# Down in 25 blocks whose lengths begin at five, its first operands asked for two groups ahead, no sum loaded at first visits, x2 added at last visits

## The chip, the cores and the metric

The kernel runs on one core of a Trainium2 chip. The metric is the device time of one execution in microseconds; lower is better. Before the change the median of three runs is 1912.93 us (1912.73 to 1913.06).

## What is computed

A decoder layer on 512 positions of width 2048, all in float32. The change is in the last line, in the product with `w_down`:

```python
D_MODEL = 2048; SEQ = 512; DEPTH = 1
D_FF = -(-(8 * D_MODEL) // (3 * 256)) * 256          # 5632
...
h = _rms_norm(x, norm1_g[l])
proj = h @ w_in[l]                                   # three head groups of token mixing
...
x = x + mix @ w_out[l]                               # x2 in the kernel
h2 = _rms_norm(x, norm2_g[l])
x = x + (jax.nn.silu(h2 @ w_gate[l]) * (h2 @ w_up[l])) @ w_down[l]
```

## The kernel before

Everything is held transposed: tiles of 128 channels x 512 positions. Four stages follow each other: the input projection, the mixers with the output projection (they leave x2 in DRAM, `x2d`, 16 tiles), gate/up, and down. Matmuls run in float32r, and each weight tile is split into a rounded part `wh` and a rest `wl`; an operand tile holds the rounded half and the rest side by side.

Gate/up and down multiply 2x2 blocks with **seven products instead of eight** (`ORDER = (5, 1, 7, 6, 2, 4, 3)`). A group is one output pair: seven products, each over a number of operand pairs `j`, each pair one `wh` matmul over 512 columns and one `wl` matmul over 256. A weight group has four raw blocks `'21'`, `'22'`, `'11'`, `'12'`; POOL adds them (L178), ACT copies the sum to PSUM (`wn`, L230) and to `wh` (L231), DVE subtracts for `wl` (L232), two products ahead of PE, with three `wh`/`wl` buffers. Four PSUM banks take the products; DVE evicts each product after it (L949, L954, L955), in `done`.

Gate/up has 44 groups (g0, u0, g1, u1, ...; pairs in the order `GU_ORDER`), eight operand pairs each; the 56 operand tiles `h` stay in SBUF. After a `u` group POOL forms sums and ACT and DVE make seven operand tiles of this pair (`piece1` to `piece4`, called in the next groups by `later`), which SP stores to DRAM (`od`). The pairs in `STAY` also stay in SBUF, and the second of them is not stored.

Down contracts over 44 row tiles, 22 pairs, for 16 output tiles (8 pairs `n` and `n + 8`). The operand tiles of all 22 pairs don't fit into the 75 slots of 128x512, so down runs as a list of **blocks** `DOWN`, each `(n, first, end)`: output pair n over operand pairs first to end - 1 (modulo 22). Before, there are 24: each n is visited three times, the window of operand pairs slides up by about one pair a block, and the list starts with lengths 6, 7, 7 and ends with seven of 7. A block's products are seven as in gate/up. At each visit SP loads the running sums of n and n + 8 (`y`, from `x2d`, so that x2 is in them from the start), DVE and POOL add the products, and SP stores the sums back to `x2d`, at the last visit to the output.

The order is written out by hand. Each engine's queue runs in the order of the program; there is no scheduler. `later(k, f, queue=extras)` puts a call at the end of the product k further on. SP issues nearly every DMA, in order: weights (`pump`, up to seven raw buffers), operands (`load_act`), sums (`load_y`), stores. A DMA into a slot waits until the slot's last reader is done, and what stands behind it on SP waits too.

Of the kernel before, what the change touches and what calls it, by code (L numbers as in the profile page):

```python
# [9 lines left out]
F32 = mybir.dt.float32  # L10
# [5 lines left out]
P = 128  # L16
T = 512
NT = T // P
D = 2048
KT = D // P  # L20
# [41 lines left out]
ORDER = (5, 1, 7, 6, 2, 4, 3)  # L62
TH = T // 2
NJ = KT // 2
NP = NF // 2


GU_ORDER = [*range(1, 6), *range(7, NP), 0, 6]
STAY = (0, 6)


_A = [0, 0, 1, 2, 3, 4, 5, 6]
_B = [_A[n] + (6 if n == 0 else 7) for n in range(8)]
_C = [b + 8 for b in _B]
DOWN = [(n, *w) for ab in (zip(_A, _B), zip(_B, _C), zip(_C, [a + NP for a in _A])) for n, w in enumerate(ab)]

LAID = (5, 7, 6, 4, 3, 1, 2)

# [35 lines left out]
def kernel(ctx: ExitStack, tc: tile.TileContext, xT, wi, wo, wgu, wd, cst_in, outT):  # L114
    nc = tc.nc
# [18 lines left out]
    def slot(name, dt=F32, cols=T):  # L134
        return sp.tile([P, cols], dt, name=name, tag="s")
# [625 lines left out]
    for name in PROJ[HEAD4:]:  # L761
        kind, what, j = name[0], name[1], name[2:]
# [3 lines left out]
        b = project(name)  # L766
# [19 lines left out]
    b = box = boxes = shared = None  # L786

    x2 = {}
# [168 lines left out]
    class Wide(Block):  # L957
# [6 lines left out]
        def done(self, q):  # L964
            if q == 1:
                self.u = slot(f"{self.name}u")
                self.u1, self.u2 = halves(self.u)
                self.both(1, self.u1)
            elif q == 7:
                self.l, self.r = slot(f"{self.name}l"), slot(f"{self.name}r")  # L970
                self.both(7, self.r[:, :TH])
                self.add(5, self.r[:, :TH], sign=nc.vector.tensor_sub)
            elif q == 6:
                self.add(6, self.u2, self.u1)
                nc.gpsimd.tensor_sub(self.r[:, :TH], self.r[:, :TH], self.u2)
# [65 lines left out]


    y = {}

    def load_y(t):
        if t < len(DOWN):
            for n in (DOWN[t][0], DOWN[t][0] + 8):
                y[t, n] = slot(f"y{t}_{n}")
                nc.sync.dma_start(y[t, n], x2d[n])

    class Down(Block):


        def __init__(self, t):
            super().__init__(f"d{t}", t % 2)
            self.n = DOWN[t][0]
            self.out = outT if t >= 16 else x2d
            self.tail = t == len(DOWN) - 1
            self.y1, self.y2 = y.pop((t, self.n)), y.pop((t, self.n + 8))

        def store(self, n, t, cols):
            def go():
# [6 lines left out]
        def done(self, q):  # L1069
            one, two = slice(0, TH), slice(TH, T)  # L1070
            if q == 1:
                self.u = slot(f"{self.name}u")
                self.u1, self.u2 = halves(self.u)
                self.both(1, self.u1)
            elif q == 7:
                self.add(7, self.y2[:, two])
                self.add(5, self.y2[:, two], sign=nc.vector.tensor_sub)
            elif q == 6:
                self.add(6, self.u2, self.u1)
                nc.gpsimd.tensor_sub(self.y2[:, two], self.y2[:, two], self.u2)  # L1080
                nc.gpsimd.tensor_sub(self.y2[:, one], self.y2[:, one], self.u2)
                nc.gpsimd.tensor_add(self.y1[:, two], self.y1[:, two], self.u2)
                self.u = self.u1 = self.u2 = None
                self.store(self.n + 8, self.y2, two)
            elif q != 5:
                t, n, cols = {2: (self.y1, self.n, one), 4: (self.y2, self.n + 8, one), 3: (self.y1, self.n, two)}[q]
                self.add(q, t[:, cols])
                self.store(n, t, cols)

    def load_act(q, pairs):  # L1090
        for j in pairs:
            if (q, j) in acts or j == STAY[1]:
                continue
            acts[q, j] = slot(f"a{q}_{j}", F32R)
            at = LAID.index(q)
            nc.sync.dma_start(acts[q, j].bitcast(F32), od[j % NP][:, at * T:(at + 1) * T])

    blk = gate = None
    for g in range(2 * NP + len(DOWN)):
        t = g - 2 * NP  # L1100
        if t < 0:
            p, m = GU_ORDER[g // 2], g % 2
            blk = Wide(p, m, gate if m else None)
            gate = blk if m == 0 else None
        else:
            n, first, end = DOWN[t]
            blk = Down(t)
        for i, q in enumerate(ORDER):
# [24 lines left out]
            run(extras)  # L1133
# [85 lines left out]
```

## Time and profile before

| | us |
|---|---|
| median of three runs | 1912.93 |
| the profiled execution, its own time | 1913.02 |
| its span, first to last instruction | 1911.2 |
| PE busy | 1889.6 |
| DVE, ACT, POOL busy | 1441.7, 1323.7, 1165.1 |
| down, from its first matmul to its last | 1469.25 to 1907.5 |

Lines are those of the kernel before. In a row `wl<-w('s', 'd0')_14950,wn`, d0 is the first down block, g6 and u6 the last gate and up group, 's' the buffer of the weight sum; `a` is an operand tile of down, `out` a PSUM bank, `y` a running sum. L941 is the matmul of gate/up and down.

### The profile page before, as it was taken

To read this page: it belongs to the slowest core of one execution; us is meant where nothing else is said; L and a number is where in the kernel's file an instruction comes from. 1 tells how busy PE (TensorE), PEld (TensorE's weight loads), DVE (VectorE), ACT (ScalarE), POOL (GpSimd) and SP (SyncE) were. 2 spreads that over 40 slices of the span, in tenths; PEclk is the share of its full clock that TensorE was granted. 3 is DMA by queue.
4 is the path that set the end of the run, shared out by engine and by line. 5 is a ranking of instruction groups with operands and counts; after the bars stand their busy time and mean duration, and the time that the engine had idled before them with its cause. 6 is when DMAs were issued, how large, how long until landed. Compare 5 with 4: busy or idle time off the path is not lost.

```text
span 1911.2 us, 29738 instructions
## 1 busy us (share of the span) xinstructions
PE 1889.6 (99%) x10332; PEld 1639.4 (86%) x10332; DVE 1441.7 (75%) x2408; ACT 1323.7 (69%) x1836; POOL 1165.1 (61%) x794
## 2 busy tenths in 40 slices
PE   8999999999999999999999999999999999999999
PEld 7888888878887888888888888888888788888888
DVE  6788888896469777777777777777777677767776
ACT  6355654454356888888878888888887677767675
POOL 5134423331056888787878878787876666556564
PEclk9999999999999999999999999999999999999999
DMA  7233333333442344454434444444438788777685
GB/s 266 85 127 93 89 103 96 94 89 118 136 144 83 127 162 148 142 179 139 175 128 165 166 160 144 153 167 146 168 127 299 271 286 281 248 261 262 211 270 195
DMA packets 135974, 320.29 MB, mean 168 GB/s; under 512 B 15504, under 2 KB 30992, under 8 KB 135824
## 3 DMA queue, kind: packets, MB, share of 16 engines
q1 hardware_dynamic: 135680, 318.30, 49.1%
q8 instruction: 81, 1.33, 0.3%
q14 instruction: 69, 0.57, 0.1%
q10 hardware_dynamic: 144, 0.10, 0.0%
HBM read 255.42 MB, written 55.31 MB: 163 GB/s over the span
## 4 chain that ended last, share of the span: by engine, by line
PE 96%; DMA 2%; DVE 1%; POOL 1%; issue 0%; SPq 0%; ACT 0%; POOLq 0%; ACTq 0%; DVEq 0%
PE out L941 66%; PE o L249 3%; PE o L251 3%; PE o L250 3%; PE cq L249 2%; PE cq L251 2%; PE cq L250 2%; PE ak L249 1%; PE ak L251 1%; PE ak L250 1%; PE av L251 1%; PE av L249 1%; PE av L250 1%; PE aq L249 1%; PE aq L250 1%; PE aq L251 1%
## 5 line engine op out<-in xcount | busy, mean ns | idle before, releaser
L941 PE MATMUL out<-h,wh 128*128 128x512 f32 x2464 | 590.2, 391 | 0.9 <-DVE h L809 0.9
L941 PEld LDWEIGHTS out<-h,wh 128*128 128x128 f32 x2464 | 453.7, 189 | 89.1 <-DVE h L809 1.4
L941 PEld LDWEIGHTS out<-h,wl 128*128 128x128 f32 x2464 | 316.1, 191 | 12.1
L941 PE MATMUL out<-h,wl 128*128 128x256 f32 x2464 | 320.0, 283 | 0.0
L941 PE MATMUL out<-a,wh 128*128 128x512 f32 x1232 | 297.8, 392 | 4.0 <-DMA a<-od 2.8
L941 PEld LDWEIGHTS out<-a,wh 128*128 128x128 f32 x1232 | 226.3, 189 | 49.8 <-DMA a<-od 5.0
L226 ACT CAST wh<-w 128x1024 fp32r<-128x1024 f32 (+1 forms) x93 | 96.9, 1042 | 121.3 <-PE o L250 52.6
L941 PEld LDWEIGHTS out<-a,wl 128*128 128x128 f32 x1232 | 160.2, 192 | 8.1 <-DMA a<-od 1.5
L941 PE MATMUL out<-a,wl 128*128 128x256 f32 x1232 | 163.0, 284 | 0.9 <-DMA a<-od 0.9
L227 DVE TENSOR_TENSOR wl<-w,wh 128x1024 fp32r<-128x1024 f32 (+1 forms) x93 | 116.0, 1247 | 54.0 <-ACT wh L226 52.1
L954 DVE TENSOR_TENSOR y<-y,out 128x256 f32<-128x256 f32 x120 | 50.5, 421 | 63.4 <-PE out L941 60.4
L426 DVE SCALAR_TENSOR_TENSOR y<-bu,cst,y 128x511 f32<-128x511 f32 (+14 forms) x120 | 89.8, 749 | 0.6
L955 DVE TENSOR_TENSOR y<-y,out 128x256 f32<-128x256 f32 x120 | 50.5, 421 | 4.1
L250 PE MATMUL o<-ml_c,wh 128*128 128x512 f32 x128 | 50.3, 393 | 2.5 <-DVE ml_c L740 2.5
L249 PE MATMUL o<-mh_c,wh 128*128 128x512 f32 x128 | 51.5, 402 | 0.0
L249 PE MATMUL cq<-hh,wh 128*128 128x512 f32 x128 | 51.2, 400 | 0.0
L251 PE MATMUL o<-mh_c,wl 128*128 128x512 f32 x128 | 50.2, 392 | 0.0
L251 PE MATMUL cq<-hh,wl 128*128 128x512 f32 x128 | 50.0, 391 | 0.0
L250 PE MATMUL cq<-hl,wh 128*128 128x512 f32 x128 | 49.9, 390 | 0.0
L836 POOL TENSOR_TENSOR ta<-h 128x256 f32<-128x256 f32 x8 | 7.3, 908 | 58.5 <-issue 44.9
L348 POOL TENSOR_TENSOR ssum<-ssum,sq 128x512 f32<-128x512 f32 x15 | 25.1, 1675 | 21.9 <-ACT sq L347 21.4
L654 POOL TENSOR_SCALAR a3e<-a3e,a3d 128x128 f32<-128x128 f32 (+3 forms) x8 | 9.1, 1150 | 36.8 <-DVE a3d L652 27.3
(3097 smaller groups left out, 4958.8 us busy)
## 6 DMA issues: line engine op xcount, KB each, us to landing
a<-od SPq DMA_DIRECT2D x182, 256.0 KB, 5.3
od<-a SPq DMA_DIRECT2D x147, 256.0 KB, 3.2
w<-in_wi SPq DMA_DIRECT2D x59, 512.0 KB, 3.7
w<-in_wo SPq DMA_DIRECT2D x32, 512.0 KB, 3.6
y<-x2d SPq DMA_DIRECT2D x48, 256.0 KB, 5.2
x2d<-y SPq DMA_DIRECT2D x64, 128.0 KB, 3.2
x<-in_xT SPq DMA_DIRECT2D x16, 256.0 KB, 7.0
xr<-in_xT SPq DMA_DIRECT2D x16, 256.0 KB, 3.7
```

The lines of the kernel that those rows point to most:

```text
L226: nc.scalar.copy(hi[:, :n], t[:, :n])
L227: eng.tensor_sub(lo[:, :n], t[:, :n], hi[:, :n].bitcast(F32))
L249: nc.tensor.matmul(out, wh, xh, start=start, stop=False)
L250: nc.tensor.matmul(out, wh, xl, start=False, stop=False)
L251: nc.tensor.matmul(out, wl, xh, start=False, stop=stop)
L348: eng.tensor_add(acc, acc, sq)
L426: nc.vector.scalar_tensor_tensor(yconv[j][:, i:], hconv[j][:, :T - i], c, yconv[j][:, i:], op0=ALU.mult, op1=ALU.add)
L654: nc.gpsimd.tensor_scalar(e[:, o:o + n], e[:, o:o + n], rd[:, i:i + 1], None, op0=ALU.mult)
L836: eng.tensor_sub(n1, h11, h12)
L941: nc.tensor.matmul(out, lhs[:, s], rhs, start=begin, stop=last and low == flip[0] and x is xs[-1], skip_group_check=True)
L954: sign(out, out if first is None else first, main)
L955: sign(out, out, rest)
```

## The change

It replaces the list of blocks, and what is loaded, added and stored with them.

- `DOWN` has 25 blocks: (0,0,5), (1,0,6), (2,0,7), (3,0,8), (4,1,9) to (7,4,12), then eight of length 8 from (0,5,13) to (7,12,20), then (0,13,18), (3,16,22), (2,15,22), (1,14,22), (4,17,23) to (7,20,26) of six, and (0,18,22) of four. n = 0 is visited four times. The pairs summed over are the same 176.
- The order is no longer a sliding window, so `FROM` and `UP_TO` say which operand pairs are still or already needed at each block. The operands of 24 pairs are loaded instead of 26.
- The first block has five operand pairs, of which pair 0 stays. Its loads for products 5 and 1 are asked in the gate group before the last (`t == -2`), the others one product after another in the last one; the last of them falls into d0's first product.
- A first visit loads no sum; its evictions write the sum tiles. Sums between visits are in DRAM tiles of their own (`yd`). At a last visit SP loads x2 as well, and POOL adds it to the loaded sum, called at the block's second product.
- `piece2` of each gate/up pair is called one product later. `STAY` is (0, 5), and `GU_ORDER` ends with 0, 5.

The diff, without what only renames:

```diff
+_A = [0, 0, 0, 0, 1, 2, 3, 4]
+_B = [n + 5 for n in range(8)]
+_C = [n + 13 for n in range(8)]
...
+DOWN += [(0, 13, 18), *((n, 13 + n, NP + _A[n]) for n in (3, 2, 1, 4, 5, 6, 7)), (0, 18, NP)]
+FROM = [min(w[1] for w in DOWN[t:]) for t in range(len(DOWN))]
+UP_TO = [max(end, 21 if n == 0 and 13 <= first else 0) for n, first, end in DOWN]
...
-                                     (5, self.piece2), (8, self.piece4)):
+                                     (6, self.piece2), (8, self.piece4)):
...
     def load_y(t):
         if t < len(DOWN):
-            for n in (DOWN[t][0], DOWN[t][0] + 8):
-                y[t, n] = slot(f"y{t}_{n}")
-                nc.sync.dma_start(y[t, n], x2d[n])
+            k = DOWN[t][0]
+            for n in (k, k + 8):
+                if t > FIRST[k]:
+                    y[t, n] = slot(f"y{t}_{n}")
+                    nc.sync.dma_start(y[t, n], yd[n])
+                if t == LAST[k]:
+                    x2[n] = slot(f"x2_{n}")
+                    nc.sync.dma_start(x2[n], x2d[n])
...
-            self.out = outT if t >= 16 else x2d
+            self.out = outT if t == LAST[self.n] else yd
...
+            if t == LAST[self.n]:
+                for n, into in zip(pair, (self.y1, self.y2)):
+                    later(1, nc.gpsimd.tensor_add, into, into, x2.pop(n), queue=extras)
...
             elif q == 7:
-                self.add(7, self.y2[:, two])
+                if self.first:
+                    self.both(7, self.y2[:, two])
+                else:
+                    self.add(7, self.y2[:, two])
...
+                if not self.first:
+                    nc.gpsimd.tensor_sub(self.y2[:, one], self.y2[:, one], self.u2)
+                    nc.gpsimd.tensor_add(self.y1[:, two], self.y1[:, two], self.u2)
...
+            if t == -2 and i in (3, 6):
+                load_act(ORDER[i // 6], range(*DOWN[0][1:]))
             if t == -1:
                 for j in range(NJ):
                     ops.pop((q, j))
-                later(1, load_act, q, range(*DOWN[0][1:]), queue=extras)
+                if i < len(ORDER) - 2:
+                    later(1 if i < len(ORDER) - 3 else 3, load_act, ORDER[i + 2], range(*DOWN[0][1:]), queue=extras)
             elif 0 <= t < len(DOWN) - 1:
-                for j in range(first, DOWN[t + 1][1]):
+                for j in range(FROM[t], FROM[t + 1]):
                     acts.pop((q, j))
-                later(1, load_act, q, range(end, DOWN[t + 1][2]), queue=extras)
+                later(1, load_act, q, range(UP_TO[t], UP_TO[t + 1]), queue=extras)
```

On SP, between the weights of the last up group and those of d0, before (a5_0 is the operand tile of product 5, pair 0; od0 its DRAM tile):

```order
L213 DMA w('12', 'u6')_14694<-in_wgu 128x1024
L915 DMA od0_5893<-a3_0_14679 128x512
L915 DMA od0_5893<-a1_0_14682 128x512
L915 DMA od0_5893<-a5_0_14745 128x512
L915 DMA od0_5893<-a7_0_14748 128x512
L915 DMA od0_5893<-a6_0_14807 128x512
L915 DMA od0_5893<-a4_0_14810 128x512
L213 DMA w('21', 'd0')_14851<-in_wd 128x768
```

and now:

```order
L921 DMA od0_5893<-a1_0_14698 128x512
L1128 DMA a5_1_14759<-od1_5894 128x512
L1128 DMA a5_2_14761<-od2_5895 128x512
L1128 DMA a5_3_14763<-od3_5896 128x512
L1128 DMA a5_4_14765<-od4_5897 128x512
L921 DMA od0_5893<-a5_0_14769 128x512
L921 DMA od0_5893<-a7_0_14772 128x512
L1128 DMA a1_1_14854<-od1_5894 128x512
L1128 DMA a1_2_14856<-od2_5895 128x512
L1128 DMA a1_3_14858<-od3_5896 128x512
L1128 DMA a1_4_14860<-od4_5897 128x512
L219 DMA w('21', 'd0')_14881<-in_wd 128x640
```

Eight operand loads have moved ahead of d0's weights, and the stores of a6_0 and a4_0 behind them. The loads of d0's product 3 (a3_1 and on) stand behind d1's '21', '22' and '11' in both.

On ACT, while d0 and the start of d1 run, before (u6ta and u6tb are sums of the last pair; wn and wh the copies of a weight):

```order
L230 CAST wn407_15232<-w('s', 'd0')_14950 128x768
L231 CAST wh407_15230<-w('s', 'd0')_14950 128x768
L230 CAST wn408_15255<-w('s', 'd1')_15188 128x896
L231 CAST wh408_15253<-w('s', 'd1')_15188 128x896
L1016 CAST u6n2_15271<-u6tb_15136 128x512
L1020 CAST a6_6_15273<-u6tb_15136 128x256
L1020 CAST a4_6_15276<-u6tb_15136 128x256
L230 CAST wn409_15284<-w('11', 'd1')_15111 128x896
L231 CAST wh409_15282<-w('11', 'd1')_15111 128x896
```

and now:

```order
L236 CAST wn407_15217<-w('s', 'd0')_14978 128x640
L237 CAST wh407_15215<-w('s', 'd0')_14978 128x640
L236 CAST wn408_15237<-w('s', 'd1')_15182 128x768
L237 CAST wh408_15235<-w('s', 'd1')_15182 128x768
L236 CAST wn409_15256<-w('11', 'd1')_15113 128x768
L237 CAST wh409_15254<-w('11', 'd1')_15113 128x768
L1022 CAST u5n2_15270<-u5tb_15134 128x512
L1026 CAST a6_5_15272<-u5tb_15134 128x256
L1026 CAST a4_5_15275<-u5tb_15134 128x256
```

The weight copies are shorter by one pair, and `piece2` stands one product later.

On POOL, at the last visit of n = 2 (d18 in both), before:

```order
L1082 TENSOR_TENSOR y17_1_18407<-y17_1_18407,d17u_18546 128x256
L178 TENSOR_TENSOR w('s', 'd18')_18573<-w('s', 'd18')_18573,w('11', 'd18')_18505 128x896
L178 TENSOR_TENSOR w('s', 'd18')_18573<-w('s', 'd18')_18573,w('12', 'd18')_18554 128x896
L178 TENSOR_TENSOR w('s', 'd19')_18769<-w('21', 'd19')_18693,w('22', 'd19')_18696 128x896
L178 TENSOR_TENSOR w('21', 'd19')_18693<-w('21', 'd19')_18693,w('11', 'd19')_18699 128x896
```

and now (L921 is the line that runs a queued call):

```order
L1103 TENSOR_TENSOR y17_3_18383<-y17_3_18383,d17u_18511 128x256
L184 TENSOR_TENSOR w('s', 'd18')_18533<-w('s', 'd18')_18533,w('11', 'd18')_18473 128x896
L921 TENSOR_TENSOR y18_2_18557<-y18_2_18557,x2_2_18559 128x512
L921 TENSOR_TENSOR y18_10_18561<-y18_10_18561,x2_10_18563 128x512
L184 TENSOR_TENSOR w('s', 'd18')_18533<-w('s', 'd18')_18533,w('12', 'd18')_18519 128x896
```

Two additions of x2 have come in between the two later sums of this block's weights.

More of the change, by code (lines that the diff above doesn't have):

```diff
@@ L65 @@
 NP = NF // 2
[L68 to L75, printed above, removed]
+GU_ORDER = [*range(1, 5), *range(6, NP), 0, 5]
+STAY = (0, 5)
+_A = [0, 0, 0, 0, 1, 2, 3, 4]
+_B = [n + 5 for n in range(8)]
+_C = [n + 13 for n in range(8)]
+DOWN = [(n, *w) for ab in (zip(_A, _B), zip(_B, _C)) for n, w in enumerate(ab)]
+DOWN += [(0, 13, 18), *((n, 13 + n, NP + _A[n]) for n in (3, 2, 1, 4, 5, 6, 7)), (0, 18, NP)]
+FROM = [min(w[1] for w in DOWN[t:]) for t in range(len(DOWN))]
+UP_TO = [max(end, 21 if n == 0 and 13 <= first else 0) for n, first, end in DOWN]
+UP_TO = [max(UP_TO[:t + 1]) for t in range(len(DOWN))]
+LAST = {n: t for t, (n, _, _) in enumerate(DOWN)}
+FIRST = {n: t for t, (n, _, _) in reversed([*enumerate(DOWN)])}
 LAID = (5, 7, 6, 4, 3, 1, 2)
@@ L1043 @@
     y = {}
+    yd = {n: tc.dram_tile([P, T], F32, name=f"yd{n}") for n in range(KT)}
     def load_y(t):
         if t < len(DOWN):
-            for n in (DOWN[t][0], DOWN[t][0] + 8):
-                y[t, n] = slot(f"y{t}_{n}")
-                nc.sync.dma_start(y[t, n], x2d[n])
+            k = DOWN[t][0]
[6 more added lines that the diff above has]
+                    nc.sync.dma_start(x2[n], x2d[n])
     class Down(Block):
@@ L1056, in __init__ @@
             self.n = DOWN[t][0]
-            self.out = outT if t >= 16 else x2d
+            self.out = outT if t == LAST[self.n] else yd
             self.tail = t == len(DOWN) - 1
-            self.y1, self.y2 = y.pop((t, self.n)), y.pop((t, self.n + 8))
+            self.first = t == FIRST[self.n]
+            pair = (self.n, self.n + 8)
+            self.y1, self.y2 = [slot(f"y{t}_{n}") if self.first else y.pop((t, n)) for n in pair]
+            if t == LAST[self.n]:
+                for n, into in zip(pair, (self.y1, self.y2)):
+                    later(1, nc.gpsimd.tensor_add, into, into, x2.pop(n), queue=extras)
         def store(self, n, t, cols):
@@ L1080, in done @@
                 nc.gpsimd.tensor_sub(self.y2[:, two], self.y2[:, two], self.u2)
-                nc.gpsimd.tensor_sub(self.y2[:, one], self.y2[:, one], self.u2)
-                nc.gpsimd.tensor_add(self.y1[:, two], self.y1[:, two], self.u2)
-                self.u = self.u1 = self.u2 = None
+                if not self.first:
+                    nc.gpsimd.tensor_sub(self.y2[:, one], self.y2[:, one], self.u2)
+                    nc.gpsimd.tensor_add(self.y1[:, two], self.y1[:, two], self.u2)
+                    self.u = self.u1 = self.u2 = None
                 self.store(self.n + 8, self.y2, two)
@@ L1086, in done @@
                 t, n, cols = {2: (self.y1, self.n, one), 4: (self.y2, self.n + 8, one), 3: (self.y1, self.n, two)}[q]
-                self.add(q, t[:, cols])
+                out = t[:, cols]
+                if not self.first:
+                    self.add(q, out)
+                elif q == 2:
+                    self.both(q, out)
+                elif q == 3:
+                    self.add(q, out, self.u2)
+                    self.u = self.u1 = self.u2 = None
+                else:
+                    main, rest = halves(self.banks[q])
+                    nc.vector.tensor_sub(out, main, self.u2)
+                    nc.vector.tensor_add(out, out, rest)
                 self.store(n, t, cols)
@@ L1091, in load_act @@
         for j in pairs:
-            if (q, j) in acts or j == STAY[1]:
+            if j in STAY or (q, j) in acts:
                 continue
```

## The prediction

> **What bounds the kernel now.** I read the page first, then the waits of PE, the stage by windows, the chain, and SP's timeline. PE is busy almost the whole span, so only its idle time and its slow stretches can be won.
>
> ```profile
> span 1911.2 us, 29738 instructions
> PE 1889.6 (99%) x10332; PEld 1639.4 (86%) x10332; DVE 1441.7 (75%) x2408; ACT 1323.7 (69%) x1836; POOL 1165.1 (61%) x794
> ```
>
> The waits of PE from 1400 us on, which is the end of gate/up and all of down, are two rows:
>
> ```profile
> PE out L941 <- DMA a<-od: 3.7, 8, 2.1
> PE out L941 <- ACT wh L231: 1.1, 1, 1.1
> ```
>
> Both lie in the first two down blocks. The windows (length, busy time and count of PE, PEld, DVE, ACT and POOL, then granted clock, DMA share, GB/s) show d0 with d1, the blocks d3 to d23, and the tail:
>
> ```profile
> 1469.25:1510.26 41.01, 36.10 (x184) 29.40 (x182) 26.67 (x47) 27.14 (x39) 23.73 (x19) 0.96 0.82 297
> 1527.30:1907.50 380.20, 380.20 (x2186) 335.59 (x2184) 272.70 (x418) 262.12 (x289) 226.70 (x144) 1.00 0.74 253
> 1907.50:1911.20 3.70, 0.01 (x1) 0.00 (x0) 0.84 (x2) 0.00 (x0) 0.00 (x0) 0.78 0.11 35
> ```
>
> Blocks d3 to d23 hold 156 operand pairs: 380.20 / 156 = 2.437 us a pair (seven products of 0.348 us), with PE never idle, in blocks of seven pairs as of eight. So a block has no cost of its own on PE. At that rate the 13 pairs of d0 and d1 need 31.7 us; they take 41.0. The loss is **9.3 us**, and only 4.9 of it is idle (41.01 less 36.10). The rest is slow work:
>
> ```profile
> 1480.90:1484.40 3.50, 2.75 (x10) 1.73 (x10) 0.51 (x2) 0.00 (x0) 0.00 (x0) 1.00 1.03 401
> 1489.70:1495.50 5.80, 4.71 (x22) 3.95 (x20) 2.31 (x5) 2.97 (x6) 4.80 (x5) 0.71 0.17 59
> 1486.50 0.50 PE L941 MATMUL out<-a,wh 128*128 128x512 f32 x1 [2.08 <-DMA a<-od]
> ```
>
> In 1489.70:1495.50 the granted clock is 0.71: (1 - 0.71) x 5.8 = 1.7 us lost. The other 2.7 us are matmuls that ran singly, each as its operand landed (2.75 us for ten). The Trainium skill (TensorE: Matmul & The Clock Gate, HAM oscillation) says PE drops to half clock after idle gaps of over about 3.4 us. Here the longest gap is 2.08 us and the clock fell; by the page's rule the recoverable loss would be 1.7 us less, by the row it is 9.3.
>
> Why d0 waits is in SP's timeline and the DMA window 1453:1491:
>
> ```profile
> 1452.10 0.33 SPq L213 DMA_DIRECT2D w('21', 'd0')_14851<-in_wd  x1
> 1453.48 2.29 SPq L1096 DMA_DIRECT2D a<-od  x5
> 1462.91 14.42 SPq L1096 DMA_DIRECT2D a<-od  x20
> 1477.70 0.33 SPq L213 DMA_DIRECT2D w('21', 'd1')_15107<-in_wd  x1
> 1479.74 3.02 SPq L1096 DMA_DIRECT2D a<-od  x5
> DMA packets 7055, 14.06 MB, mean 370 GB/s; under 512 B 782, under 2 KB 909, under 8 KB 7052
> a<-od SPq DMA_DIRECT2D x35, 256.0 KB, 5.4
> 1469.25:1480.90 11.65, 11.37 (x64) 9.52 (x62) 9.94 (x19) 9.14 (x15) 4.54 (x4) 1.00 1.05 389
> ```
>
> The DMA engines are full for 38 us (share 1.05, 389 GB/s). The last products' operands come late, and d1's weights, asked behind them at 1477.70, come later still; so POOL's sum, ACT's copy and PE's 1.1 us wait follow.
>
> **The change, part by part.**
>
> *Fewer and earlier operands.* d0 needs 28 loads (pairs 1 to 4) instead of 35. Eight of them are asked one group earlier, before d0's weights. The four y loads of d0 and d1 go, since first visits load no sum. That is 19 x 0.262 MB = 5.0 MB out of the full stretch, 12.8 us at 389 GB/s. What SP still asks from 1452.1 on (d0's weights 1.3 MB, 16 loads and three od stores 5.0 MB) is 6.3 MB or 16.2 us: it ends near 1470, 1 us after d0's start. I take all 9.3 us as won.
>
> *What is late next in d0: operand 3.* Its four loads stay behind d1's first three weights. These wait for the split of d0's third product, at about 1.8 us of the block (w('21', 'd22') below is asked about 2.1 us into d21: 1858.37, three blocks of 17.06 us before 1907.50 being 1856.3). Three weights of 384 KB and four loads are 2.2 MB, 5.8 us at 389 GB/s, and a load into an idle queue takes some 2 us more than its bytes:
>
> ```profile
> w('21', 'g6')_14437<-in_wgu SPq DMA_DIRECT2D x1, 512.0 KB, 3.3
> ```
>
> 3.3 us, of which 1.3 are 512 KB at 389 GB/s. So 1.8 + 2 + 5.8 = 9.6 us. The product starts at 6 x 1.74 = 10.4. Just in time: I take 0.2, ends 0 and 3.
>
> *What is late next in d0: ACT and DVE.* The operand pieces of the last gate/up pair are made while d0 runs. Rows of d0 and d1 (768 and 896 columns):
>
> ```profile
> L231 ACT CAST wh<-w('s', 'd0')_14950 128x768 fp32r<-128x768 f32 x2 | 1.7, 829 | 0.0
> L230 ACT CAST wn<-w('s', 'd0')_14950 128x768 fp32r<-128x768 f32 x2 | 1.6, 798 | 1.3 <-DVE wl L232 1.3
> L231 ACT CAST wh<-w('s', 'd1')_15188 128x896 fp32r<-128x896 f32 x2 | 1.9, 936 | 0.0
> L1016 ACT CAST u6n<-u6ta 128x512 fp32r<-128x512 f32 x1 | 0.6, 581 | 0.0
> L1020 ACT CAST a<-u6ta 128x256 fp32r<-128x256 f32 x2 | 0.7, 402 | 0.0
> L232 DVE TENSOR_TENSOR wl<-w('s', 'd0')_14950,wn 128x768 fp32r<-128x768 f32 x3 | 2.8, 948 | 0.4 <-PE out L941 0.4
> L949 DVE TENSOR_REDUCE u6r<-out 128x256 f32<-128x512 f32 x2 | 1.4, 692 | 1.3 <-PE out L941 1.3
> L955 DVE TENSOR_TENSOR y<-y,out 128x256 f32<-128x256 f32 x5 | 2.1, 420 | 0.2
> ```
>
> 128 columns are worth 0.107 us of an ACT copy, so a five-pair split costs ACT 0.69 + 0.72 = 1.41 us. In d0's 12.2 us ACT has five of these, two of d1 (1.63 each) and three pieces (0.58 + 2 x 0.40 = 1.39): 14.5 us, 2.3 too many. DVE has seven splits (about 5.9), evictions (4.6, and 0.8 of the group before) and six subtractions of 0.42: 13.8, 1.6 too many. The split runs two products ahead, a cover of 2 x 1.74 less 0.72 and 0.81 of copy and subtraction, about 1.9 us. Followed product by product, the seventh product of d0 waits 0.5 us and two of d1 0.2 and 0.4; then d1's 14.6 us (12.6 of ACT) catch up. I take 1.1, ends 0 and 2.3. The moved piece spreads ACT's work away from a Silu in the same step; from 1400 us on gate/up has no PE wait (the rows above), and the piece's result is wanted three products later at the soonest: 0.
>
> *First visits.* A reduction of 0.69 us stands for two additions (0.84), and two of POOL's three subtractions go. DVE and POOL are not waited for in these blocks: 0.
>
> *Last visits.* 16 loads of x2 and 16 POOL additions of 128x512, two a block. The nearest row has the shape; the second shows where POOL would run them:
>
> ```profile
> L994 POOL TENSOR_TENSOR u6r<-u6r,g6r 128x512 f32<-128x512 f32 x1 | 1.3, 1299 | 1.9 <-DVE u6r L949 1.9
> 1859.88 2.14 POOL L178 TENSOR_TENSOR w('s', 'd21')_19161<-w('s', 'd21')_19161,w('12', 'd21')_19142 128x896 f32<-128x896 f32 x1 [4.26 <-ACT wh L231]
> ```
>
> 2 x 1.3 = 2.6 us go into an idle 4.3 us ahead of that sum, so neither the sum nor DVE's first addition to y (after the third product) is moved: 0, if x2 has landed.
>
> *Short late blocks: transfers.* (0,13,18) has 12.2 us in which SP asks a six-pair block's weights (1.57 MB), seven operands (1.83), two y, two x2 (1.05) and stores (0.52): 4.98 MB. Three six-pair blocks, from (4,17,23) on, ask as much in 14.6 us each. Nearest rows, both of about 5.0 MB:
>
> ```profile
> 1632.07:1651.57 19.50, 19.50 (x115) 17.23 (x114) 13.57 (x20) 13.02 (x14) 11.77 (x7) 1.00 0.73 256
> 1856.16:1873.23 17.07, 17.07 (x100) 15.07 (x99) 12.64 (x20) 11.67 (x14) 10.64 (x7) 1.00 0.86 292
> 1858.37 0.81 SPq L213 DMA_DIRECT2D w('21', 'd22')_19281<-in_wd  x2
> 1861.17 0.47 SPq L1096 DMA_DIRECT2D a<-od  x1
> ```
>
> Busy time 0.73 x 19.50 = 14.2 us and 0.86 x 17.07 = 14.7; at 389 GB/s it would be 12.8. So (0,13,18) runs 0.6 to 2 us late, and the two blocks after it load no operand and catch up; a six-pair block is at most 0.1 late. The cover: operand 3 is asked at 1861.17, 4.9 us into its block, lands some 5.4 later and is wanted after six products of 2.44, 14.6 us: 4.3 to spare, 2.2 with six pairs. I take 0.5 for all, ends 0 and 3. The Trainium skill (DMA: Bandwidth & Descriptors, Specifications) gives a core about 358 GB/s from HBM. By it (0,13,18) takes 13.9 us and I would write 1.6 for this term; 389 GB/s over 11.65 us says the limit is higher here.
>
> *Last block and tail.* Four pairs, 9.75 us; DVE has five splits of 0.67 and 5.7 us of evictions, 9.1. It fits, and what follows the last matmul (3.70 us) is the same two additions and store: 0.
>
> **Sum.** 1911.2 - 9.3 + 1.1 + 0.2 + 0.5 = 1903.7 us of span. The profiled run took 1913.02, 1.8 above its span: **1905.5 us**. The median of 1912.93 is 0.1 under that run, which I leave out. The gain is 0.39%; this kernel's measurement tells about 0.2% (3.8 us) from no change.
>
> **Rivals.**
>
> *The wait moves to operand 3 in d0* (chance 0.14). Its margin above is under 1 us. If DVE and ACT free the raw buffer 3 us later than I think, PE waits over 2 us, and the half clock (1.7 us) comes back with the wait: 1905.5 + 3.5 = 1909. For it: the loads stay behind three weights. Against: SP's queue is empty by then.
>
> *Slower: the late short blocks run out of transfers* (0.07). Where four blocks ask 5 MB in 12 to 15 us, a lateness beyond the 2.2 us of cover stops PE, and each stop of 2 us costs 1.7 more by the clock: 1903.7 + 4 x 3.7 = 1918.5 and 1.8 for the run, near 1920. It decides once a block's DMA work passes about 17 us. For it: share 0.86 already. Against: 38 us at share 1.0 in the transition.
>
> *The change doesn't do what it says* (0.04): slots free so late in the group before that SP stands at the early loads and the weights behind them are late; then the 9.3 us are lost in gate/up instead, 1912 to 1914. Against: at d0 SP's loads wait for products already done, since each product frees eight slots and four are taken.
>
> **How the numbers follow.** The likeliest case has 0.75 and its own range 1903.7 (all new terms 0) to 1907.3. The range reaches over most of the first rival: 1903.4 to 1909.0. Faster by over 0.2% (under 1909.1): 0.75 and half of 0.14 and a little, 0.83. Within 0.2%: the other half and half of the third, 0.09. Slower: 0.08.
>
> **What would show it.** Right: in the changed profile PE has no wait for a<-od of over 1 us in d0, no clock under 1.00 between the two stages, d1's first weight is asked about 2 us into d0, and down takes about 431 us instead of 438. The 1.1 us would show as waits for ACT wh or DVE wl in d0 and d1. Wrong: waits for a<-od in (3,16,22) or after (4,17,23), or a clock of 0.5 there.

## The result, and the profile after

| | before | after |
|---|---|---|
| median of four runs, us | 1912.99 (1912.73 to 1914.52) | 1904.76 (1903.87 to 1905.51) |
| profiled execution, us | 1913.02 | 1905.27 |
| down, first to last matmul, us | 438.26 | 428.99 |

The ratio is 0.9953, 95% interval 0.9941 to 0.9965: faster by 0.47%. The page after opens with

```profile
span 1903.5 us, 29681 instructions
PE 1886.3 (99%) x10332; PEld 1638.7 (86%) x10332; DVE 1443.3 (76%) x2412; ACT 1326.4 (70%) x1850; POOL 1179.6 (62%) x801
```

PE's longest waits, over the whole span, are now

```profile
PE in L255 <- ACT wh L232: 5.3, 1, 5.3
PE o L256 <- DVE ml_c L746: 3.1, 3, 2.5
PE n2s L295 <- DVE ssum L100: 2.0, 1, 2.0
PE out L947 <- DVE h L815: 0.9, 1, 0.9
```

No row of a<-od, of ACT wh at L237 or of DVE wl at L238 is left: from 1400 us to the end PE has no wait at all. Windows of after: all of down, its first two blocks, and the start of gate/up (columns as in the prediction):

```profile
1470.76:1899.75 428.99, 428.99 (x2465) 378.75 (x2463) 315.60 (x489) 304.19 (x356) 274.91 (x177) 1.00 0.74 255
1470.76:1482.95 12.19, 12.19 (x71) 10.75 (x70) 11.11 (x22) 11.06 (x19) 10.08 (x9) 1.00 0.81 282
1482.95:1497.60 14.65, 14.65 (x87) 12.92 (x85) 13.17 (x22) 12.64 (x20) 9.23 (x7) 1.00 0.63 223
600.00:640.00 40.00, 37.06 (x193) 32.07 (x192) 31.51 (x43) 29.83 (x43) 24.83 (x18) 0.91 0.28 97
```

and of before:

```profile
1469.25:1907.51 438.26, 433.35 (x2465) 380.05 (x2463) 312.36 (x485) 301.79 (x342) 262.18 (x170) 1.00 0.75 259
600.00:640.00 40.00, 37.06 (x199) 31.69 (x198) 32.70 (x44) 31.26 (x44) 26.25 (x18) 0.96 0.30 108
```

Down is 9.27 us shorter, and every block now runs at 2.436 us a pair: the 176 pairs need 428.8 us and took 429.0. But down begins 1.51 us later (1470.76 against 1469.25). This comes from gate/up's start, before anything that the change touches: the same wait of 2.0 us there was followed by 3.4 us of half clock (granted clock 0.5) in the profile before and by 6.8 us in this one (0.96 and 0.91 above). Both lengths come with either list of blocks: 6.8 us in e3 below, which has the old list, and 3.4 us in e2, which has the new one. 1911.2 - 9.27 + 1.51 is 1903.4, and the span is 1903.5. Since such a half clock comes and goes from run to run, the experiments are compared by the length of down in their profile, the run times beside it.

SP's timeline around d0, after:

```profile
1472.64 0.33 SPq L219 DMA_DIRECT2D w('21', 'd1')_15109<-in_wd  x1
1473.02 0.42 SPq L219 DMA_DIRECT2D w('22', 'd1')_15111<-in_wd  x1
1473.54 0.38 SPq L219 DMA_DIRECT2D w('11', 'd1')_15113<-in_wd  x1
1474.01 2.07 SPq L1128 DMA_DIRECT2D a<-od  x4
```

d1's first weight is asked 1.9 us into d0 (8.45 us before), and SP is no longer stuck in a row of operand loads.

### The profile page after: what moved, and what is told of

Same layout as the page of the kernel before. It is cut to its first block, busy times and chain, and to the rows that moved or that the text cites. A ratio compares the mean times of both kernels' runs of the same rounds, so it can differ in the third digit from the quotient of the medians.

```text
span 1903.5 us, 29681 instructions
## 1 busy us (share of the span) xinstructions
PE 1886.3 (99%) x10332; PEld 1638.7 (86%) x10332; DVE 1443.3 (76%) x2412; ACT 1326.4 (70%) x1850; POOL 1179.6 (62%) x801
## 4 chain that ended last, share of the span: by engine, by line
PE 97%; DVE 2%; DMA 1%; issue 0%; SPq 0%; POOL 0%; ACT 0%; POOLq 0%; ACTq 0%; DVEq 0%
PE out L947 67%; PE o L256 3%; PE o L255 3%; PE o L257 3%; PE cq L255 2%; PE cq L257 2%; PE cq L256 2%; PE ak L255 1%; PE ak L257 1%; PE ak L256 1%; PE av L255 1%; PE av L256 1%; PE av L257 1%; PE aq L255 1%; PE aq L256 1%; PE aq L257 1%
## 5 line engine op out<-in xcount | busy, mean ns | idle before, releaser
L960 DVE TENSOR_TENSOR y<-y,out 128x256 f32<-128x256 f32 x93 | 39.1, 420 | 43.4 <-PE out L947 37.9
L961 DVE TENSOR_TENSOR y<-y,out 128x256 f32<-128x256 f32 x101 | 42.5, 421 | 3.5
```

The source lines that it names most:

```text
L960: sign(out, out if first is None else first, main)
L961: sign(out, out, rest)
```

## Experiments

The theory: in d0, operands and d1's weights stand in one queue on SP. The loss of before is the lateness of the last of them, with the half clock that the wait brings, and each load taken out of the queue wins its share. The rival: one part of the change won it all.

All eight combinations of the three parts, where "list" is the new list of blocks with the moved piece, "early" the loads asked earlier (not by the same edit in both lists, as told below), "no sums" the missing sums at first visits with x2 added at last. "Lost" is down's length less 428.8 us; "asked" is when d1's first weight is asked, us into d0, from SP's timeline; "half" is the length of half clock within down, by the clock's records; all from the profiles, in us.

| list | early | no sums | run | median, us | down | lost | asked | PE waits | half |
|---|---|---|---|---|---|---|---|---|---|
| | | | before | 1912.99 | 438.26 | 9.5 | 8.45 | 4.8 | 3.4 |
| | yes | | e3_before_early | 1915.02 | 439.62 | 10.8 | 8.24 | 7.0 | 6.8 |
| | | yes | e4_before_nosum | 1910.94 | 435.76 | 7.0 | 6.91 | 2.5 | 6.8 |
| | yes | yes | e9_early_nosum | 1910.93 | 435.56 | 6.8 | 7.00 | 3.9 | 6.8 |
| yes | | | e5_list_alone | 1911.36 | 436.79 | 8.0 | 6.22 | 3.6 | 3.4 |
| yes | | yes | e1_late_ask | 1908.92 | 435.04 | 6.2 | 4.70 | 1.9 | 6.8 |
| yes | yes | | e2_sums_loaded | 1905.67 | 430.66 | 1.9 | 1.87 | 1.0 | 0 |
| yes | yes | yes | after | 1904.76 | 428.99 | 0.2 | 1.88 | 0 | 0 |

Ratios to before: e3 1.0007 (0.9997 to 1.0016), e4 0.9987 (0.9977 to 0.9996), e9 0.9990 (0.9981 to 1.0000), e5 0.9990 (0.9981 to 1.0000), e1 0.9976 (0.9967 to 0.9985), e2 0.9957 (0.9943 to 0.9972). A stretch of 3.4 us at half clock costs 1.7 us of work, so where one row has 3.4 and the other 6.8, 1.7 us of the difference in "lost" can be that alone.

**e3_before_early**, the kernel before with

```diff
+            if t == -2 and i == 6:
+                load_act(ORDER[0], range(*DOWN[0][1:]))
...
-                later(1, load_act, q, range(*DOWN[0][1:]), queue=extras)
+                if i < len(ORDER) - 1:
+                    later(1, load_act, ORDER[i + 1], range(*DOWN[0][1:]), queue=extras)
```

> The kernel before with one edit: the first loads of each operand are asked one product earlier than before, the first operand's in the group before the last. Theory (transfers decide): five loads (3.4 us) leave the short stretch, so the 9.3 us lost in the first two blocks become 4 to 6, down 433 to 435 us. Rival (asking early alone is what won it): most of the 9.3 us goes, down below 431 us. Second rival (the loads wait for their buffers or their stores and asking earlier changes nothing): down 438 us.

Missed by the theory's own number: nothing is won. PE's waits in down, POOL's wait in d0 to d2, and SP's timeline of e3:

```profile
PE out L941 <- DVE wl L232: 4.7, 1, 4.7
PE out L941 <- ACT wh L231: 2.3, 1, 2.3
```

```profile
POOL w('s', 'd1')_15188 L178 <- DMA w('22', 'd1')_15119<-in_wd: 9.4, 1, 9.4
```

```profile
1475.99 1.67 SPq L1096 DMA_DIRECT2D a<-od  x3
1478.03 0.33 SPq L213 DMA_DIRECT2D w('21', 'd1')_15117<-in_wd  x1
```

The operands are in time now (no a<-od row). But all 35 loads now stand ahead of d1's weights, where before the last five stood behind them, so the weights are asked as late as before; POOL waits for block '22', and its sum, ACT's copies and DVE's subtraction pass that on to PE. In before, POOL waited just as long:

```profile
POOL w('s', 'd1')_15188 L178 <- DMA w('22', 'd1')_15109<-in_wd: 9.6, 1, 9.6
```

So before had two late things in one queue, and taking one away only showed the other.

**e4_before_nosum** is the kernel before with the `load_y` and the first and last visits of the change, and **e9_early_nosum** is e4 with the edit of e3:

```diff
-            for n in (DOWN[t][0], DOWN[t][0] + 8):
-                y[t, n] = slot(f"y{t}_{n}")
-                nc.sync.dma_start(y[t, n], x2d[n])
+            k = DOWN[t][0]
+            for n in (k, k + 8):
+                if t > FIRST[k]:
...
+                if t == LAST[k]:
```

> The kernel before with one edit: no sum is loaded at first visits, x2 is added at last visits. Theory (transfers decide): four loads of 256 KB (2.7 us) leave the stretch, so the 9.3 us lost in the first two blocks become 5 to 7, down 434 to 436 us. Rival (the sums' loads have no part in it, since they are asked behind the a loads that are waited for): down stays at 438 us. Second rival (they alone fill the queues): down below 431 us.

> The kernel before with both of its separate edits: operand loads one product earlier, and no sum loaded at first visits, x2 added at last. Alone the first was worth about -1 us in down, the second +2.5. Theory (one queue; the first edit only let the second block's weights, which stand behind all the operands, be the last instead of the last operand's loads): now those weights are asked 1.4 us earlier than in the first edit (the two sums of the first block are out of the way) and the sums of the second block are behind them anyway; the wait for the weights becomes 5 to 6 us instead of 7.0, the clock still falls: loss 7 to 9 us, down 436 to 438 us. Rival (the two edits add): down 437 us with a wait for a loads. Second rival (together they empty the queue in time, and the clock stays up): loss under 3 us, down below 432 us.

e4 is as the theory has it: four loads (2.7 us) fewer, 2.5 us won, and the late operands still there (PE's waits in down):

```profile
PE out L943 <- DMA a<-od: 2.5, 3, 2.1
```

In e9 the wait for the weights is again what is left (PE's waits):

```profile
PE out L943 <- DVE wl L234: 3.5, 1, 3.5
PE out L943 <- ACT wh L233: 0.4, 1, 0.4
```

The mechanism is the expected one, the size is not: the weights are asked 1.2 us earlier in the block than in e3 and the waits shrink by 3.1 us, more than I allowed. Nor do the two edits add (that would be 437.1 us).

**e5_list_alone** and **e1_late_ask** are the changed kernel with

```diff
-            if t == -2 and i in (3, 6):
-                load_act(ORDER[i // 6], range(*DOWN[0][1:]))
...
-                if i < len(ORDER) - 2:
-                    later(1 if i < len(ORDER) - 3 else 3, load_act, ORDER[i + 2], range(*DOWN[0][1:]), queue=extras)
+                later(1, load_act, q, range(*DOWN[0][1:]), queue=extras)
```

and e5 besides with x2 loaded as the sum at first visits (the edit of e2). **e2_sums_loaded** is the changed kernel with

```diff
-                if t > FIRST[k]:
-                    y[t, n] = slot(f"y{t}_{n}")
-                    nc.sync.dma_start(y[t, n], yd[n])
...
+                y[t, n] = slot(f"y{t}_{n}")
+                nc.sync.dma_start(y[t, n], yd[n] if t > FIRST[k] else x2d[n])
...
-            self.first = t == FIRST[self.n]
+            self.first = False
```

> The changed kernel with its early asking undone and with x2 loaded as the sum at first visits: of the change only the new list of blocks is left (five pairs first) and the moved piece. Seven operand loads fewer must land before the second block than in the kernel before. Theory as the first runs left it (operands and the second block's weights stand in one queue, and the loss is the lateness of the last of them, with 1.7 or 3.4 us of half clock on top): seven loads are 4.8 us, the clock still falls; loss in the first three blocks 6 to 8.5 us against 9.0 before, down about 435 to 437.5 us, with waits for a loads. Rival (the shorter first block is what mattered): loss under 4 us, down under 433 us. Second rival (a shorter first block gives the transfers less time and takes back what it saves): 9 us or more, down 438 us.

> The changed kernel with its early asking undone: each operand's first loads are asked one product after its product of the last up group, as in the kernel before. Theory (the 9.3 us in the first two down blocks were lost because too many transfers had to land there, so each edit wins its share): the list and the missing sums already take 7 loads (4.8 us at 0.68 us each) out of that stretch, so 1.5 to 4.5 us come back in down (431 to 434 us against 429.0 in the changed kernel and 438.3 before), with waits for a loads in the first down block. Rival (asking early alone is what won the time): about 9 us come back, down near 438 us. Second rival (the list and the sums alone won it): down stays at 429 us.

> The changed kernel, but with x2 loaded as the sum at first visits, as before, and no x2 added at last visits. Four more loads of 256 KB (2.7 us of transfers) must land in the first blocks of down. Theory (transfers decide, and operand 3's loads in the first block landed only 0.8 us ahead of their use): 0.5 to 1.5 us longer in down, as a wait of the fourth operand's products of the first block. Rival (the sums were what delayed the a loads before, whatever the order): 3 us or more. Second rival (with loads asked two groups ahead nothing is short any more): within 0.2 us in down.

The row in which each loses most, of e5, e1 and e2:

```profile
PE out L947 <- DMA a<-od: 2.8, 5, 1.8
```

```profile
PE out L947 <- DMA a<-od: 1.9, 1, 1.9
```

```profile
PE out L947 <- DVE wl L238: 1.0, 2, 0.7
```

e5 lies within the theory's 435 to 437.5 us, e1 a us above its 434. e2's size (1.7 us more than the changed kernel) is a little over its 1.5, and the wait is at another place than I said: not for operand 3, whose last load landed as it was wanted, but for DVE in d1 and d2. A first visit that adds to a loaded sum gives POOL three operations on the sums (0.7 us each) instead of one. In d1 ACT's third piece waits for sums behind them, and DVE's additions wait for them, each with the next weight's work behind it (ACT's and DVE's waits in e2):

```profile
ACT u5n L1022 <- POOL u5tb L1017: 2.0, 1, 2.0
DVE y L960 <- POOL y L1095: 3.3, 3, 1.6
```

POOL begins the third piece's sums 12.7 us after d0's first matmul, against 10.7 in the changed kernel: 0.6 us by a later landing of block '22', 1.4 by the two operations more. So the price of the loaded sums is not one of transfers alone.

What follows: no part won the 9.3 us alone. Asking early is worth nothing with the old list (-1.4 and +0.2 us in down) and 6.0 to 6.1 us with the new one. But the two ways of asking early differ: e3 and e9 ask one product earlier and move all 35 loads ahead of d1's weights; the changed kernel asks two products earlier and holds the last four loads back, so that these weights stand behind 24 loads, eight of them asked before d0's weights. How much of the 6 us is the new list's and how much this order's is not shown: no run has the changed kernel's order with the old list.

**e8_piece_back**, the changed kernel with

```diff
-                                     (6, self.piece2), (8, self.piece4)):
+                                     (5, self.piece2), (8, self.piece4)):
```

> The changed kernel with the second piece of each gate/up pair back at its place, one product earlier. Theory (it was put at no cost and no gain): gate/up and down the same within 0.2 us. Rival (with the five-pair block ACT has 0.5 us to spare, and the earlier piece takes it): a wait for ACT or DVE of 0.5 to 1.5 us in the first down block, down 429.5 to 430.5 us.

Gate/up did not change, but down took 429.91 us: d1 lost 0.9. PE's wait there, and ACT's timeline that shows why:

```profile
PE out L947 <- ACT wh L237: 0.6, 1, 0.6
```

```profile
1478.66 0.83 ACT L237 CAST wh<-w('s', 'd1')_15182 128x768 fp32r<-128x768 f32 x1
1481.16 0.59 ACT L1022 CAST u5n<-u5tb 128x512 fp32r<-128x512 f32 x1 [1.67 <-POOL u5tb L1017]
1481.68 0.71 ACT L1026 CAST a<-u5tb 128x256 fp32r<-128x256 f32 x2
1482.30 0.80 ACT L236 CAST wn<-w('11', 'd1')_15113 128x768 fp32r<-128x768 f32 x1
```

The earlier piece stands at the head of ACT's queue and waits 1.67 us for POOL's sum, and d1's next weight copy behind it waits too. The theory's "no gain" was wrong; the rival had the size, but not the place (it said d0) nor the way (it spoke of ACT's time, not of a wait for POOL). The run time (1904.72 us, ratio 0.9955, 0.9938 to 0.9971) does not show 0.9 us.

**e6_act_more**, the changed kernel with

```diff
+            if t == 0 and i < 6:
+                if i == 0:
+                    spare = slot("spare")
+                    nc.gpsimd.memset(spare, 0.0)
+                nc.scalar.copy(spare, spare)
```

> The changed kernel with six more ACT copies of a spare 128x512 tile (0.5 to 0.6 us each), one behind each of the first six products of the first down block. In the changed kernel ACT was busy 11.1 of that block's 12.2 us and a copy of the weights was ready 0.5 us ahead of its product at the end. Theory (ACT has about 1 us to spare in the block, since its instructions overlap: copies of 0.69 us start every 0.63 us): 3.2 us of copies give waits for ACT or DVE of 1 to 2.5 us in the first two blocks, and perhaps 1.7 us of half clock; down 430 to 433 us. Rival (the sum made from durations, by which ACT was already 2.3 us short and the cover took it): the shortage becomes 5.5 us and waits of 3 us or more follow, down over 432 us. Second rival (ACT is not what the start of down hangs on): within 0.2 us of 429.0.

Down took 432.20 us (1906.76, ratio 0.9969, 0.9957 to 0.9981): 2.5 us lost in d0, 0.6 in d1, waits of 0.9 for ACT wh and 0.9 for DVE wl, no half clock. ACT's timeline:

```profile
1472.13 0.62 ACT L1172 COPY spare<-spare 128x512 f32<-128x512 f32 x1 [1.68 <-POOL spare L1171]
1472.66 0.69 ACT L236 CAST wn<-w('s', 'd0')_14978 128x640 fp32r<-128x640 f32 x1
1473.28 0.72 ACT L237 CAST wh<-w('s', 'd0')_14978 128x640 fp32r<-128x640 f32 x1
1473.91 0.61 ACT L1172 COPY spare<-spare 128x512 f32<-128x512 f32 x1
```

ACT was held up by six copies of 0.52 us, start to start, and by 1.68 us in which the first waited for the tile to be cleared, which I had not counted: 4.8 us, of which PE lost 3.1. So ACT has about 1.7 us of room at the start of down in the changed kernel. By durations it would have been 2.3 us short before these copies.

**e7_dma_four** and **e7_dma_two**, the changed kernel with x2 of the lower tile loaded four or two times more at each last visit:

```diff
+                    if n < NJ:
+                        for again in range(4):
+                            nc.sync.dma_start(slot(f"x2_{n}_{again}"), x2d[n])
```

> The changed kernel with four more loads of 256 KB at each last visit (x2 of the lower output tile again, not used): 2.7 us of transfers more for each of the late blocks, which in the changed kernel kept the DMA engines busy for 13.8 to 14.5 us of their 14.6. So three or four of the six-pair blocks ask for 16.5 to 17.2 us of transfers in 14.6 us. Theory (lateness adds up from block to block and shows once it passes the 2 to 4 us for which operands are ahead): the blocks (5,18,24) to (7,20,26) end up about 5 us late, 2 to 3 us of waits for a loads, and 1.7 to 3.4 us of half clock; down 431 to 435 us. The slower rival of the prediction (past about 17 us of transfers a block each such block stops): four stops of 3.7 us, down near 444 us. Second rival (transfers have more room than that): no wait, down 429 us.

> The changed kernel with two more loads of 256 KB at each last visit instead of four: 1.4 us of transfers more for each of the late blocks, so the six-pair blocks ask for about 15 to 16 us of transfers in 14.6 us. With four more loads four blocks lost 1.3, 1.4, 1.5 and 6.1 us. Theory (lateness adds up and shows only past the cover, and the smallest cover in the changed kernel, from an operand's landing to its use in (3,16,22), is 1.7 us): at most one short wait, 0 to 0.7 us in down, no half clock; down 429 to 429.7 us. Rival (transfers already limit the late blocks, so the price goes with the bytes): half of the 10.3 us, down about 434 us.

With four, down took 439.27 us (1910.66, ratio 0.9987, 0.9978 to 0.9996; the profiled run was the longest of ten). Blocks (3,16,22), (2,15,22), (6,19,25) and (7,20,26) lost 1.3, 1.4, 1.5 and 6.1 us, half clock of 6.8 us in the last. Its waits in down:

```profile
PE out L947 <- DMA a<-od: 4.3, 3, 2.3
PE out L947 <- DVE wl L238: 1.5, 2, 1.0
```

That is between the theory (431 to 435) and the prediction's slower rival (444), with the rival's four stops. With two, down took 430.86 us (1906.02, ratio 0.9960, 0.9945 to 0.9975); the theory allowed 0.7 us, and 1.9 were lost, in the first two of these blocks. Windows of (3,16,22) and (2,15,22), PE's wait, and POOL's:

```profile
1777.93:1793.09 15.16, 15.02 (x87) 12.79 (x85) 10.99 (x19) 8.71 (x13) 10.11 (x7) 1.00 1.01 359
1793.09:1811.49 18.40, 17.41 (x98) 15.20 (x99) 14.22 (x24) 15.27 (x18) 16.65 (x14) 1.00 0.77 277
```

```profile
PE out L947 <- DVE wl L238: 1.0, 1, 1.0
```

```profile
POOL w('s', 'd18')_18537 L184 <- DMA w('22', 'd18')_18475<-in_wd: 3.7, 1, 3.7
POOL y L921 <- DMA x<-x2d: 1.2, 1, 1.2
```

The DMA engines are full in (3,16,22) (share 1.01). That block lost 0.5 us, of which an operand's late landing is only 0.1; the rest stands at its end, where PE turns to the next block's first weight just as ACT's copy of it ends. ACT's timeline:

```profile
1791.25 0.91 ACT L236 CAST wn<-w('s', 'd18')_18537 128x896 fp32r<-128x896 f32 x1 [4.28 <-POOL w('s', 'd18')_18537 L184]
1792.09 0.94 ACT L237 CAST wh<-w('s', 'd18')_18537 128x896 fp32r<-128x896 f32 x1
```

POOL's sum came late because block '22' did (3.7 us of wait, 2.1 in the changed kernel), and the next weight cost PE another 1.0. (POOL's own wait of 1.2 us for x2 came earlier, and POOL then stood idle for '22' all the same.) So nearly all of it is the weights behind the loads; I had reckoned with the operands' slack (1.7 us) and not with the weights'.

**e10_norm_later** and **e11_fill_gap** leave down as it is and go at the half clock at gate/up's start. e10 calls `norm2a` and `norm2b` one product later; e11 fills PE's wait:

```diff
-            if g == 0 and i in (2, 3):
-                (norm2a, norm2b)[i - 2]()
+            if g == 0 and i in (3, 4):
+                (norm2a, norm2b)[i - 3]()
```

```diff
+        for wh, x in fill:
+            nc.tensor.matmul(n2["b"][:, T:], wh[:, :P], x, start=True, stop=True)
...
+                (norm2a, norm2b)[i - 2](*[(w[0], ops[q, j]) for j in range(NJ)])
```

> The changed kernel with one edit outside down: the eight small matmuls n2s of the second norm, which wait 2.0 us for DVE's ssum at the start of gate/up, are called one product later, and what follows from them as well. In every profile so far this gap of 2.0 us was followed by a half clock of 3.4 or 6.8 us, as were gaps of 1.8 to 4.7 us in down, while gaps of up to 1.1 us were not. Theory (the gap is what brings the half clock): gap and half clock go together, 2.0 plus 1.7 or 3.4 us, so 1899.5 to 1901.5 us against 1904.8 of the changed kernel. Rival (the norm's result is then late for the first gate product that needs it, and the wait moves there): 1904 to 1907 us. Second rival (the half clock at this place has another cause than the gap): the gap goes, the half clock stays, about 1903 us.

> The changed kernel with eight matmuls of 128x512 on operands that lie in SBUF (their products are overwritten, unused) put ahead of the norm's n2s matmuls, so that PE works through the 2.0 us for which it waits there for DVE's ssum. Nothing else is moved: the eight take about 1.85 us, and ssum is ready 2.0 us after they can start. Theory (a half clock follows where PE idled for over half of a stretch of 3.4 us; the gap of 2.0 us brings it, whatever is waited for): no half clock near 618 us; the first gate group, from the first matmul on h to the 113th, takes about 24.2 us instead of the 25.9 or 27.3 us that it took with 3.4 or 6.8 us of half clock; span about 1900 us where the other two half clocks come as before, time 1901.5 to 1903.5 us. Rival (the half clock at this place has another cause, for instance the eight n2s matmuls of one column each, which keep PE nearly empty for 1.9 us): it stays, and the time is 1904 to 1906 us.

e10 fell to its rival, though the wait has another releaser than I said (1906.16 us, ratio 0.9962, 0.9947 to 0.9977; PE's waits):

```profile
PE n2s L295 <- DVE wl L238: 3.8, 1, 3.8
```

A likely reading, which no run shows: n2s takes one of the two PSUM buffers that weight copies pass through, and one product later it queues behind DVE's reading of such a copy.

e11 came out as the theory had it: 1902.49 us (1901.37 to 1902.89 in five runs), ratio 0.9940 (0.9927 to 0.9954), the fastest version here. PE's timeline and the window at gate/up's start:

```profile
615.54 2.00 PE L907 MATMUL n2s<-h,wh 128*128 128x512 f32 x8
617.74 1.05 PE L295 MATMUL n2s<-ones,ssum 128*128 128x1 f32 x8 [0.19 <-DVE ssum L100]
618.65 1.20 PE L949 MATMUL out<-h,wl 128*128 128x256 f32 x8
```

```profile
600.00:640.00 40.00, 38.87 (x214) 33.25 (x213) 34.16 (x47) 32.79 (x46) 27.91 (x19) 1.00 0.31 112
```

The clock stays at 1.00 and the first gate group takes 24.4 us instead of 27.3 (after) or 25.9 (before). Matmuls whose product nobody reads win about 2 us, because PE would otherwise idle and then run at half clock. The size rests on these profiles (1.5 or 2.9 us): the interval of the ratio overlaps that of the changed kernel (0.9941 to 0.9965).

## Why the prediction was right, and where it was not

- **The loss of 9.3 us, all won: right.** Down is 9.27 us shorter, clock 1.00 between the stages, and d1's weight is asked 1.9 us into d0 (forecast 1.8). That it was the queue of transfers is shown by the eight combinations, in which the loss falls, roughly, with the time at which d1's weights are asked, and by POOL's waits for block '22'; what each part is worth by itself is not shown for "early". The sum for SP's requests has a slip that changes nothing behind it: 16.2 us from 1452.1 end at 1468.3, not near 1470. The prediction named the weights behind the operands only as what follows from the late operands; e3 and e9 show that they are a second cause, at least as large as the first (waits of 7.0 us in e3, 3.7 us for operands in before).
- **ACT and DVE short, 1.1 us: mis-sized, it is 0.** The step that failed is the sum of ACT's work in d0, in two ways. Of the 14.5 us, 2.1 did not run there: the third piece (1.39) stands behind d1's fourth copy, in the order shown ahead of the prediction, and one copy (0.69) ran before d0 began. The other 12.4 us are a sum of durations, and instructions that follow each other overlap, so ACT was busy for 11.1 us. In the rows of e6 a copy of 640 columns lasts 0.69 or 0.72 us and the next begins 0.62 or 0.63 after its start. The Trainium skill (ScalarE: Activation LUTs, What ACT_TABLE_LOAD costs) says that back-to-back ACTIVATEs overlap by about 93 ns, near the 0.07 to 0.09 us of these copies. DVE was busy for 11.1 us, where 13.8 were counted; its durations in d0 add up to 12.2. The limit is near all the same: e6 finds some 1.7 us of room.
- **The moved piece, 0: mis-sized.** It is worth 0.9 us in d1 (e8). I looked at when its result is wanted, not at what stands behind it in ACT's queue.
- **Operand 3 in d0, 0.2 us: 0.** Its last load landed 0.8 us ahead of its use, by the trace. "Just in time" was right, and the first rival did not come.
- **Late short blocks, 0.5 us: 0.** No operand there is wanted sooner than 1.7 us after its landing. The second rival is a real mechanism, but its point, 17 us of transfers a block, was too high: in e7_dma_two 1.9 us were lost at a share of 1.01 in a block of 15.2 us. A full block alone is not the point either, since three later blocks of that run, at shares of 1.02 to 1.05, lost nothing; where the point lies stays open.
- **x2's additions, the last block, the tail: right within 0.2.** The last block took 0.17 us over its rate, the tail 3.73 us (3.71 before).
- **The half clock.** Against the Trainium skill (TensorE: Matmul & The Clock Gate, HAM oscillation) I took a gap of about 2 us to be enough. e11 shows it: filling one of 2.0 us removes the half clock. What I left out is that the same gap is followed by 3.4 or 6.8 us of half clock from run to run, which cost the first gate group 1.5 or 2.9 us against e11.

The span came within 0.2 us of the sum, 1903.7. That is partly luck: 1.8 us of new terms did not come, and 1.5 us of clock at gate/up's start did.

## What to carry to other kernels

Where several late things stand in one in-order queue, price the whole queue: curing the first in line only shows the next, and a cure that wins nothing while another late thing stands in the queue can win once that is gone. Sum an engine's work by the time from start to start, not by durations, count only what runs in the stretch, and look at what stands behind a moved instruction as well as at who wants its result. On PE a wait of about 2 us cost up to 2.9 us more in clock here, so filling such a wait with unread matmuls can pay.

## What the runs showed of the hardware

I cut the 14 profiles into stretches of 3.413 us along each one's own grid of clock events (in the profile before, the half clocks begin at 417.9, 619.3 and 1489.7: 59 and 255 stretches apart) and summed PE's idle time in each stretch between 30 and 1890 us that ran at full clock. All 25 stretches with 1.9 us of idle or more were followed by half clock; of 33 with 0.8 to 1.38 us all but one were not (that one, in before, holds matmuls that ran singly, whose ends are modelled); between 1.39 and 1.87 it went both ways, eight without and six with. So it is not the longest gap that counts, but the idle time in a fixed stretch. The same gap of 2.47 us shows it: in after it lies across two stretches and no half clock follows; in before most of it lies in one. Windows of after, then of before (the first number behind the length is PE's busy time):

```profile
412.27:415.68 3.41, 2.20 (x13) 1.60 (x11) 3.38 (x9) 3.39 (x6) 0.31 (x1) 1.00 0.00 0
415.68:419.09 3.41, 1.85 (x9) 1.37 (x10) 3.41 (x6) 1.13 (x3) 2.56 (x1) 1.00 0.46 92
```

```profile
414.49:417.90 3.41, 1.23 (x7) 0.86 (x8) 3.41 (x6) 1.32 (x3) 2.87 (x1) 1.00 0.22 36
```

The Trainium skill (TensorE: Matmul & The Clock Gate, What's actually happening) says that the window is 3413 ns and free-running, and this agrees. What stays open is what decides between 1.39 and 1.87 us, and why a half clock lasts one stretch in some runs and two in others.
